# A fp32 transformer block on one Trainium2 core: a seventh-product form for three of eight k pairs in the feed-forward part

## The chip, the cores and the metric

The program runs on one core of one Trainium2 chip. The time is the device time of one execution in microseconds (us). Before the change three runs gave 1486.8, 1486.99 and 1487.1 us (median 1486.99). The profile is of one execution more, of 1487.96 us.

The engines are named as the profile names them: PE (matmuls; PEld is its weight load), DVE (elementwise on two operands), ACT (copies, casts, functions), POOL (here a few small operations and some transfers), SP (here only the queue of weight loads).

## The reference

One layer of a streaming encoder, all in fp32, for x of 256 x 2048 (256 tokens):

```
h = RMSNorm(x);  proj = h @ w_in                     # 2048 x 10240: q, k, v twice, two gates
y_sb = stick_breaking_attention(...)                  # 8 heads of 128
y_ca = chunked_relpos_attention(...)                  # 8 heads of 128
x += (sigmoid(g_sb) * (y_sb @ w_sb_out) + sigmoid(g_ca) * (y_ca @ w_ca_out)) @ w_mix_out
h = RMSNorm(x);  g, u = split(h @ w_ffn_in)           # 2048 x 11264
x += (silu(g) * u) @ w_ffn_out                        # 5632 x 2048
x += sigmoid(RMSNorm(x) @ w_ple_gate) * (p @ w_ple_in)
out = RMSNorm(x)
```

The change touches the two feed-forward products alone, `h @ w_ffn_in` and `(silu(g) * u) @ w_ffn_out`.

## The kernel before, in words

**How fp32 is kept.** PE multiplies in a reduced format (fp32r). Every fp32 operand is split into two tiles, hi (a cast) and lo (the rest), and a product is three matmuls, hi by hi, hi by lo and lo by hi (`three`, L254 to L256). A weight tile `raw` of 128 x 1024 (two k tiles of 128 rows by 512 columns, one transfer of 512 KB) comes in on SP's queue; ACT makes hi from it (L225) and DVE makes lo (L207, the helper `minus`). There are five raw buffers (`RAW`), and four pairs of hi and lo in the feed-forward part. The activations stand as tables of transposed tiles, T1, T2, T3, with hi and lo of each k tile.

**The feed-forward part** is cut into units. A unit multiplies all k tiles of a table with two weight blocks of 512 columns: for w_ffn_in the gate and the up columns of one group of 512 hidden features (16 k tiles, 8 pairs), for w_ffn_out two neighbouring groups of 512 output columns. The hidden features go in blocks (`FF_BLOCKS`, 16, 16 and 12 k tiles of 128): four, four and three units of w_ffn_in, each block followed by two units of w_ffn_out over its 16, 16 or 12 k tiles (8, 8 or 6 pairs). That makes 17 units. An ordinary pair has two weight blocks, two k tiles and two halves of the tokens: 8 products, 24 matmuls of 128 x 512.

**The 7-product form.** For the pairs in `PAIRS` (numbers 2 and 4 of each unit) the two k tiles and the two weight blocks are taken as a 2 x 2 matrix of blocks, and the eight products are replaced by seven of sums of blocks (`pair_products`), 21 matmuls. The price: DVE forms four sums of raw tiles, 128 x 512 each, (`split_pair`, written to `xf` and once in place to `raw`), ACT casts the three of them that are in xf (128 x 1536, L246), DVE takes their rest (`T<-xf,T`). The activation side needs the corresponding sums once per table (`forms` in `into_table`: four DVE additions `fm` of 128 x 128, a cast, a rest). Three of the seven products go straight into the unit's four result banks; four go into banks of their own, `su` (q1, q5, q6, q7). When the last such pair is done, `mid` (L792, L794) puts them together in the tile C: one ACT copy and four DVE additions. At the end of each weight block the result banks are added to C (L801, or L822 and L823), with silu and the product of gate and up behind (L805 to L810). PSUM has eight banks: four for the results of a unit and four for its su; the next unit swaps them, so its first results go to the banks that `mid` empties.

**Order.** The code records pieces in program order (`prefetch`, `split`, `products`): weights are loaded as far ahead as raw buffers are free, splits run up to three pieces ahead as far as hi and lo buffers reach. Small work (transposes of finished hidden features into a table, `into_table`) is put in `tasks` and run between pieces. A scheduler that plays the program through then sets the order on each engine, so rows of different pieces stand interleaved. Each engine runs its own list in order, and waits on the others by semaphores.

**Buffers that the change names.** T1 is free in the feed-forward part: its first 6144 columns are room for the casts of xf (two halves in turn), the rest holds `F_in`, the form tiles of the table of w_ffn_in. `F_out`, those of w_ffn_out, has a buffer with the tag "gf" that later holds the final gain vector `gf`. In the last two units the room is in T3.

Of the kernel before, what the change touches and what calls it, by code (L numbers as in the profile page):

```python
# [10 lines left out]
F32R = mybir.dt.float32r  # L11
# [5 lines left out]
P = 128  # L17
# [13 lines left out]
SCALE = P**-0.5  # L31
NB = 512
FB = 256
FF_BLOCKS = [16, 16, 12]

PAIRS = (2, 4)
RAW = 5


# [1 line left out]
def block_kernel(ctx: ExitStack, tc: tile.TileContext, x, p, w_in, w_sb_out, w_ca_out, w_mix_out,  # L41
# [18 lines left out]
    nc = tc.nc  # L60
# [65 lines left out]
    pieces = []  # L126
# [23 lines left out]
    def unit(wsrc, n0s, kts, lhs, forms, ext, mid, post, needs, row0=0):  # L150

        state["unit"] = state.get("unit", -1) + 1
        pool, side = late["ps"][:: 1 if state["unit"] % 2 == 0 else -1]
        g = dict(kind="unit", post=post, mid=mid, lhs=lhs, keep=None, forms=forms, ext=ext, pool=pool, side=side)
        kts = list(kts)
        for i in range(len(kts) // 2):
            part = kts[2 * i : 2 * i + 2]
            r = (row0 + 2 * i) * P
            src = [wsrc[r : r + 2 * P, n0 : n0 + NB].rearrange("(k p) n -> p k n", p=P) for n0 in n0s]
            pc = dict(g=g, kts=part, ncol=NB, needs=[needs(kt) for kt in part])  # L160
            if i in PAIRS:
                pieces.append(dict(pc, src=src, pair=True, first=i == PAIRS[0], last=i == PAIRS[-1]))
            else:
                for b in range(2):
                    pieces.append(dict(pc, src=[src[b]], block=b, first=i == 0, last=2 * i + 2 == len(kts)))
# [157 lines left out]
    late = {}  # L323
# [41 lines left out]
    def into_table(dst, c, src, gain=None, key=None, forms=None, pool=None):  # L365
# [3 lines left out]
        for k0 in range(0, 4, n):  # L369
# [7 lines left out]
            g = None if gain is None else [gT[:, gain + kt + k : gain + kt + k + 1] for k in range(n)]  # L377
            if forms is not None and kt // 2 in PAIRS:
                af = late["pool"].tile([P, 2, S], F32, tag="af", name="af", bufs=2)
# [289 lines left out]
    for mixer, make in ((0, sb_tasks), (1, ca_tasks)):  # L669
        for b in range(2):  # L670
# [3 lines left out]
            first = mixer == 0 and b == 0  # L674
# [75 lines left out]
    lp = ctx.enter_context(tc.tile_pool(name="late", bufs=1))  # L750
# [5 lines left out]


    flat = T1.rearrange("p k c s -> p (k c s)")
    F_in = flat[:, 6144:].rearrange("p (i c f s) -> p i c f s", i=len(PAIRS), c=2, f=4)
    F_out = lp.tile([P, len(PAIRS), 2, 4, P], F32R, tag="gf", name="F")  # L760
    late["F"] = [[F[:, i] for i in range(len(PAIRS))] for F in (F_in, F_out)]

    pt = lp.tile([P, NT, D_PLE], F32, tag="af", name="pt", bufs=2)
    dma_x.dma_start(pt, p[0, 0].rearrange("(t p) d -> p t d", p=P))
# [31 lines left out]
    def in_post(dst, c, key):  # L796
        def post(g, b):
            C = g["C"]
            for t in range(NT):
                i = 2 * b + t  # L800
                nc.vector.tensor_tensor(C[:, i, :], g["ps"][i], C[:, i, :], ALU.add)  # L801
            if b == 0:
                sg = lp.tile([P, NT, NB], F32, tag="sg", name="sg")
                for t in range(NT):
                    nc.scalar.activation(sg[:, t, :], C[:, t, :], AF.Sigmoid)  # L805
                for t in range(NT):
                    nc.vector.tensor_tensor(C[:, t, :], C[:, t, :], sg[:, t, :], ALU.mult)
            else:
                for t in range(NT):
                    nc.vector.tensor_tensor(C[:, t, :], C[:, t, :], C[:, 2 + t, :], ALU.mult)  # L810
                later(lambda: into_table(dst, c, C[:, :2, :], key=key, pool=g["pool"],
                                         forms=lambda kt: late["F"][1][kt // 4 - 1]))
        return post
# [17 lines left out]
    k0 = 0  # L831
    for blk, nk in enumerate(FF_BLOCKS):
        key = f"h{blk}"
        for c in range(nk // 4):
            j = k0 // 4 + c
            unit(w_ffn_in[0], (j * NB, D_FF + j * NB), range(KD), T3, lambda kt: late["F"][0][kt // 4 - 1], T1,
                 mid, in_post(T2, c, key), lambda kt: ("ffn", kt))
        last = blk == len(FF_BLOCKS) - 1
        for c in (0, 2):
            unit(w_ffn_out[0], (c * NB, (c + 1) * NB), range(nk), T2, lambda kt: late["F"][1][kt // 4 - 1],  # L840
                 T3 if last else T1, mid, out_unit_post(c, last), lambda kt, key=key: (key, kt), row0=k0)
        k0 += nk
# [6 lines left out]
    gf = lp.tile([P, D], F32, tag="gf", name="gf")  # L849
# [104 lines left out]
```

## Time and profile before

| what | value |
|---|---|
| profiled execution | 1487.96 us, span 1486.2 us |
| median of three runs | 1486.99 us (1486.8 to 1487.1) |
| PE busy | 1467.7 us, 99% of the span |
| DVE busy | 1071.5 us, 72% |
| ACT busy | 764.0 us, 51% |
| granted PE clock | 0.998, mean of the span |
| DMA | 289.07 MB, 195 GB/s in the mean |

Busy time is the union of an engine's intervals. The duration of one instruction is longer than the distance between two starts, since instructions of PE, and those of DVE, overlap their neighbours; so a duration times a count is not time on the engine, and distances between starts are read from the timeline. Waits name the engine and instruction that ended an idle time. A window gives the busy time of each engine in a stretch of the span. The feed-forward part runs from about 673 us to 1400 us of the span.

### The profile page before, as it was taken

The numbers are of one execution on the slowest core, as the hardware profiler recorded it, in microseconds if no ns is written. First come the engines' busy times: TensorE is split into PE (matmuls) and PEld (weight loads), VectorE is DVE, ScalarE is ACT, GpSimd is POOL, SyncE is SP. The second block draws the span as 40 slices with busy tenths as digits, with TensorE's granted clock in tenths as the row PEclk, the third lists the DMA queues.
The fourth block names the chain that finished last, engine by engine and source line by source line (L and its number), as shares of the span: only waits on it lengthen the run. The fifth ranks groups of instructions, "written<-read, shape, count | busy, mean of one in ns | idle before, by whom it ended". The sixth has DMA issues, their size and how long they took to land.

```text
span 1486.2 us, 18409 instructions
## 1 busy us (share of the span) xinstructions
PE 1467.7 (99%) x6922; PEld 1224.5 (82%) x6922; DVE 1071.5 (72%) x1291; ACT 764.0 (51%) x917; POOL 24.8 (2%) x45
## 2 busy tenths in 40 slices
PE   8999999999999999999999999999999999999997
PEld 6888888888888888887888888888888888887786
DVE  6667676665444566458888888888888888888875
ACT  6455554455454444457555544455454445555552
POOL 1100000000000000000000000000000000000000
PEclk9999999999999999999999999999999999999999
DMA  8855556556666666666666566666656666656672
GB/s 267 262 172 171 174 171 186 177 168 186 191 193 194 187 189 202 195 212 201 198 186 202 186 205 212 199 198 183 200 183 199 213 200 196 194 176 197 226 230 97
DMA packets 164810, 289.07 MB, mean 195 GB/s; under 512 B 9040, under 2 KB 44160, under 8 KB 164464
## 3 DMA queue, kind: packets, MB, share of 16 engines
q1 hardware_dynamic: 162560, 278.96, 60.7%
q0 software_dynamic: 2160, 8.93, 1.8%
q8 instruction: 54, 0.88, 0.2%
q14 instruction: 36, 0.29, 0.1%
HBM read 282.09 MB, written 5.77 MB: 194 GB/s over the span
## 4 chain that ended last, share of the span: by engine, by line
PE 91%; DVE 3%; DMA 2%; ACT 1%; issue 1%; SPq 0%; POOL 0%; POOLq 0%; DVEq 0%; ACTq 0%
PE mm L254 24%; PE mm L255 24%; PE mm L256 24%; PE mm L315 8%; PE mm L317 4%; PE su L255 2%; PE su L256 2%; PE su L254 2%; DVE lo L207 1%; DMA raw<-in_w_ffn_out 1%; PE tp L374 1%; DMA pin_d<-pst 1%; DVE T L207 0%; ACT hi L225 0%; DMA x<-in_x 0%
## 5 line engine op out<-in xcount | busy, mean ns | idle before, releaser
L207 DVE TENSOR_TENSOR lo<-raw,hi 128x1024 fp32r<-128x1024 f32 (+1 forms) x517 | 629.2, 1220 | 327.7 <-ACT hi L225 325.8
L225 ACT CAST hi<-raw 128x1024 fp32r<-128x1024 f32 (+1 forms) x449 | 471.6, 1051 | 534.9 <-PE mm L256 419.8
L255 PE MATMUL mm<-lo,T 128*128 128x512 f32 x1576 | 615.7, 391 | 0.0
L256 PE MATMUL mm<-hi,T 128*128 128x512 f32 x1576 | 614.5, 392 | 0.3 <-DVE T L402 0.3
L254 PE MATMUL mm<-hi,T 128*128 128x512 f32 x1576 | 588.0, 391 | 3.8 <-ACT hi L225 2.2
L254 PEld LDWEIGHTS mm<-hi,T 128*128 128x128 f32 x1576 | 296.0, 188 | 65.9 <-ACT hi L225 3.2
L255 PEld LDWEIGHTS mm<-lo,T 128*128 128x128 f32 x1576 | 296.4, 188 | 61.6 <-DVE lo L207 0.9
L256 PEld LDWEIGHTS mm<-hi,T 128*128 128x128 f32 x1576 | 296.2, 188 | 60.8 <-DVE T L402 0.7
L315 PE MATMUL mm<-T,hi 128*128 128x512 f32 x512 | 180.4, 399 | 0.0
L317 PE MATMUL mm<-T,lo 128*128 128x256 f32 x512 | 140.8, 280 | 0.0
L315 PEld LDWEIGHTS mm<-T,hi 128*128 128x128 f32 x512 | 95.3, 188 | 21.4
L317 PEld LDWEIGHTS mm<-T,lo 128*128 128x128 f32 x512 | 96.3, 189 | 1.1
L207 DVE TENSOR_TENSOR T<-xf,T 128x1536 fp32r<-128x1536 f32 x34 | 59.5, 1751 | 4.4 <-ACT T L246 4.3
L207 DVE TENSOR_TENSOR xf<-raw 128x512 f32<-128x512 f32 x68 | 46.5, 684 | 17.5 <-DMA raw<-in_w_ffn_out 8.8
L243 ACT CAST hi<-raw 128x1024 fp32r<-128x1024 f32 x34 | 35.9, 1057 | 39.1 <-PE mm L256 26.3
L246 ACT CAST T<-xf 128x1536 fp32r<-128x1536 f32 x34 | 50.4, 1482 | 10.3 <-DVE xf L207 10.2
L794 DVE TENSOR_TENSOR C<-su,C 128x512 f32<-128x512 f32 x68 | 45.3, 687 | 11.5 <-PE su L256 9.5
L240 ACT CAST hi<-raw 128x1024 fp32r<-128x1024 f32 x34 | 36.1, 1061 | 25.1 <-PE mm L256 19.5
L801 DVE TENSOR_TENSOR C<-mm,C 128x512 f32<-128x512 f32 x44 | 29.9, 682 | 0.0
L360 ACT COPY tm<-mm 128x256 f32<-128x256 f32 x32 | 11.9, 372 | 24.2 <-PE mm L317 24.2
L255 PE MATMUL mm<-T,T 128*128 128x512 f32 (+1 forms) x66 | 24.1, 365 | 0.1
L254 PE MATMUL mm<-T,T 128*128 128x512 f32 (+1 forms) x66 | 24.1, 365 | 0.0
(223 smaller groups left out, 1045.0 us busy)
## 6 DMA issues: line engine op xcount, KB each, us to landing
raw<-in_w_ffn_in SPq DMA_DIRECT2D x176, 512.0 KB, 4.3
raw<-in_w_in SPq DMA_DIRECT2D x159, 512.0 KB, 3.6
raw<-in_w_ffn_out SPq DMA_DIRECT2D x88, 512.0 KB, 4.7
raw<-in_w_mix_out SPq DMA_DIRECT2D x32, 512.0 KB, 4.6
raw<-in_w_ple_gate SPq DMA_DIRECT2D x32, 512.0 KB, 5.0
raw<-in_w_sb_out SPq DMA_DIRECT2D x16, 512.0 KB, 4.5
raw<-in_w_ca_out SPq DMA_DIRECT2D x16, 512.0 KB, 4.2
raw<-in_w_ple_in SPq DMA_DIRECT2D x4, 512.0 KB, 4.6
```

The lines of the kernel that those rows point to most:

```text
L207: nc.vector.tensor_tensor(out, a, b, ALU.subtract)
L225: nc.scalar.copy(hi[:, c : c + m], raw[:, c : c + m])
L240: nc.scalar.copy(h1, raw1)
L243: nc.scalar.copy(h2, raw2)
L246: nc.scalar.copy(xh, xf)
L254: nc.tensor.matmul(ps, xh, hi, start=a, stop=False)
L255: nc.tensor.matmul(ps, xh, lo, start=False, stop=False)
L256: nc.tensor.matmul(ps, xl, hi, start=False, stop=z)
L315: nc.tensor.matmul(ps, hi[:, i, f], lhs[:, kt, :, :].rearrange("p c s -> p (c s)"), start=a, stop=False)
L317: nc.tensor.matmul(ps[:, :S], lo[:, i, f], lhs[:, kt, 0, :], start=False, stop=z)
L794: nc.vector.tensor_tensor(C[:, i, :], q, C[:, j, :], ALU.add)
L801: nc.vector.tensor_tensor(C[:, i, :], g["ps"][i], C[:, i, :], ALU.add)
```

## The change

`PAIRS` becomes (2, 4, 6), and a unit takes those numbers that are smaller than its last pair: 2, 4 and 6 of 8, as before 2 and 4 of 6. The blocks come in the order 12, 16, 16. The form tiles of w_ffn_in, now three, get the buffer with the tag "gf"; those of w_ffn_out lie in T1 behind its first 6144 columns (two) and in a new buffer of 4 KB per partition (the third). The scratch for descriptors of DMAs that POOL starts is set to 8192 bytes.

```diff
-FF_BLOCKS = [16, 16, 12]
-
-PAIRS = (2, 4)
+FF_BLOCKS = [12, 16, 16]
+
+PAIRS = (2, 4, 6)
...
-            if i in PAIRS:
-                pieces.append(dict(pc, src=src, pair=True, first=i == PAIRS[0], last=i == PAIRS[-1]))
+            taken = [j for j in PAIRS if j < len(kts) // 2 - 1]
+            if i in taken:
+                pieces.append(dict(pc, src=src, pair=True, first=i == taken[0], last=i == taken[-1]))
...
-    F_in = flat[:, 6144:].rearrange("p (i c f s) -> p i c f s", i=len(PAIRS), c=2, f=4)
-    F_out = lp.tile([P, len(PAIRS), 2, 4, P], F32R, tag="gf", name="F")
-    late["F"] = [[F[:, i] for i in range(len(PAIRS))] for F in (F_in, F_out)]
+    F_in = lp.tile([P, 3, 2, 4, P], F32R, tag="gf", name="F_in")
+    F_out = flat[:, 6144:].rearrange("p (i c f s) -> p i c f s", i=2, c=2, f=4)
+    F_more = lp.tile([P, 2, 4, P], F32R, tag="fo", name="F_more")
+    late["F"] = [[F_in[:, i] for i in range(3)], [F_out[:, 0], F_out[:, 1], F_more]]
...
-    nc = bacc.Bacc("TRN2", target_bir_lowering=False, num_devices=1)
+    nc = bacc.Bacc("TRN2", target_bir_lowering=False, num_devices=1, dynamic_dma_scratch_size=8192)
```

In the built programs PE has 5890 matmuls of 128 x 512 before and 5845 now. On DVE the additions that fill xf go from 68 and 34 to 98 and 49, those into raw from 34 to 49, the rests `T<-xf,T` from 34 to 49; on ACT the casts `T<-xf` go from 34 to 49. The activation side has a form step more for three tables: the additions `fm` go from 32 to 44. POOL's and SP's lists hold the same transfers; on POOL the load of `gf` now stands ahead of the first two loads of `pi` and not behind them. Line numbers of the changed kernel are one higher from about L160 on and two higher from about L760 on.

Two places show what moves. The first is DVE around `mid` (the rows `C<-su`) in a unit of w_ffn_in. `lo<-raw,hi` is the rest of an ordinary weight tile, `xf<-raw` and `raw<-raw` are sums for the next 7-product pair, `C<-mm` adds a result bank at the end of a weight block. Before:

```order
L207 TENSOR_TENSOR T_71<-xf,T_71 128x1536
L207 TENSOR_TENSOR lo<-raw,hi 128x1024 x3
L794 TENSOR_TENSOR C<-su_8041,C 128x512
L794 TENSOR_TENSOR C<-su_8042,C 128x512
L794 TENSOR_TENSOR C<-su_8040,C 128x512 x2
L207 TENSOR_TENSOR lo<-raw,hi 128x1024 x4
L801 TENSOR_TENSOR C<-mm_7942,C 128x512
L207 TENSOR_TENSOR xf<-raw 128x512
```

And in the changed program:

```order
L208 TENSOR_TENSOR T_71<-xf,T_71 128x1536
L208 TENSOR_TENSOR lo<-raw,hi 128x1024 x2
L208 TENSOR_TENSOR xf<-raw 128x512
L796 TENSOR_TENSOR C<-su_8283,C 128x512
L208 TENSOR_TENSOR raw<-raw 128x512
L796 TENSOR_TENSOR C<-su_8284,C 128x512
L803 TENSOR_TENSOR C<-mm_8175,C 128x512
L208 TENSOR_TENSOR xf<-raw 128x512
L796 TENSOR_TENSOR C<-su_8282,C 128x512 x2
L208 TENSOR_TENSOR lo<-raw,hi 128x1024
```

The four additions of `mid` have moved to the end of the unit. They stand among the sums for the next unit's first 7-product pair, one of them (`xf<-raw`, which waits for a weight tile of the next unit) in front of the first, and among the additions of the result banks.

The second place is PE from the last products into the su banks (of q6 and q7) on. `mm_7943` and `mm_8176` are result banks of the same unit. Before:

```order
L255 MATMUL su_8041<-T_71 128x512
L256 MATMUL su_8041<-T_71 128x512
L255 MATMUL su_8042<-T_71 128x512
L256 MATMUL su_8042<-T_71 128x512
L255 MATMUL mm_7943<-T_71,T_4848 128x512
L256 MATMUL mm_7943<-T_71,T_4848 128x512
L254 MATMUL mm_7943<-hi,T_4848 128x512
```

In the changed program, where `mm_8524` is the second result bank of the next unit:

```order
L257 MATMUL su_8284<-T_71,F_in 128x512
L256 MATMUL mm_8176<-T_71,T_4848 128x512
L257 MATMUL mm_8176<-T_71,T_4848 128x512
L255 MATMUL mm_8176<-hi,T_4848 128x512
L256 MATMUL mm_8176<-lo,T_4848 128x512
L257 MATMUL mm_8176<-hi,T_4848 128x512
L255 MATMUL mm_8176<-hi,T_4848 128x512
L256 MATMUL mm_8176<-lo,T_4848 128x512
L257 MATMUL mm_8176<-hi,T_4848 128x512
L255 MATMUL mm_8524<-hi,T_72 128x512
```

Before, 66 rows of the same unit stand between the last product into an su bank and the first of the next unit. Now there are eight, the rest of pair 7, before the first matmul that waits for `mid`: `mm_8524` waits for the first of the four additions, a matmul 6 places later for the second, and one 20 places later for the last.

## The prediction

> **What bounds the kernel now.** I began with the page, whose first part says PE, then asked stage by stage where PE stands still.
>
> ```profile
> PE 1467.7 (99%) x6922; PEld 1224.5 (82%) x6922; DVE 1071.5 (72%) x1291; ACT 764.0 (51%) x917; POOL 24.8 (2%) x45
> 655.00:700.00 45.00, 43.90 (x207) 35.70 (x206) 34.57 (x53) 36.51 (x59) 3.49 (x5) 1.00 0.63 204
> 700.00:1345.00 645.00, 645.00 (x2890) 534.36 (x2889) 541.81 (x624) 328.93 (x341) 0.00 (x0) 1.00 0.64 197
> 1345.00:1405.00 60.00, 56.57 (x256) 44.53 (x255) 51.87 (x72) 34.76 (x55) 2.72 (x4) 1.00 0.64 214
> ```
>
> A window's row is the stretch, its length, busy time of PE, PEld, DVE, ACT and POOL, the granted PE clock, the DMA share and GB/s. In the 645 us that hold nearly the whole feed-forward part PE is busy without a gap at clock 1.00, and DVE is busy for 541.81 us, 84%. PE stands still 1.1 us on the way in and 3.4 us on the way out. So in this stage a matmul less is time less, as long as DVE follows. What one costs is the distance between starts:
>
> ```profile
> 1032.71 0.39 PE L255 MATMUL mm<-lo,T 128*128 128x512 f32 x1
> 1032.94 0.39 PE L256 MATMUL mm<-hi,T 128*128 128x512 f32 x1
> 1033.16 0.39 PE L254 MATMUL mm<-hi,T 128*128 128x512 f32 x1
> 1033.39 0.39 PE L255 MATMUL mm<-lo,T 128*128 128x512 f32 x1
> 1024.91:1068.01 43.10, 43.10 (x196) 35.71 (x195) 37.64 (x48) 23.49 (x26) 0.00 (x0) 1.00 0.65 202
> 1161.45:1203.61 42.16, 42.16 (x187) 34.92 (x187) 35.14 (x40) 20.02 (x19) 0.00 (x0) 1.00 0.67 207
> ```
>
> Three starts lie 0.68 us apart, 0.227 us each. The last rows are one unit of w_ffn_in (with eight transposes) and one of w_ffn_out: 42.16 / 186 matmuls gives 0.2267 us again.
>
> **What is removed.** All 11 units of w_ffn_in and the four long units of w_ffn_out get one more 7-product pair, three matmuls less each: 45 x 0.2267 = **-10.2 us**. A unit of w_ffn_in then takes 43.10 - 0.68 = 42.42 us of PE, a long one of w_ffn_out 41.48.
>
> **What is added lies on DVE and ACT.** DVE's queue, where it is full, shows its prices as distances between starts:
>
> ```profile
> 1024.86 0.68 DVE L810 TENSOR_TENSOR C<-C 128x512 f32<-128x512 f32 x1
> 1025.46 1.22 DVE L207 TENSOR_TENSOR lo<-raw,hi 128x1024 fp32r<-128x1024 f32 x1
> 1026.60 1.75 DVE L207 TENSOR_TENSOR T<-xf,T 128x1536 fp32r<-128x1536 f32 x1
> 1028.26 1.22 DVE L207 TENSOR_TENSOR lo<-raw,hi 128x1024 fp32r<-128x1024 f32 x1
> 1031.74 0.28 DVE L389 TENSOR_TENSOR fm<-af 128x128 f32<-128x128 f32 x1
> 1031.94 0.28 DVE L207 TENSOR_TENSOR fm<-af 128x128 f32<-128x128 f32 x1
> 1032.14 0.68 DVE L207 TENSOR_TENSOR T<-tp,T 128x512 fp32r<-128x512 f32 x1
> 1044.47 2.81 DVE L794 TENSOR_TENSOR C<-su,C 128x512 f32<-128x512 f32 x4 [0.36 <-PE su L256]
> 1050.09 1.22 DVE L207 TENSOR_TENSOR lo<-raw,hi 128x1024 fp32r<-128x1024 f32 x1 [1.05 <-ACT hi L225]
> 1052.81 1.22 DVE L207 TENSOR_TENSOR lo<-raw,hi 128x1024 fp32r<-128x1024 f32 x1 [1.50 <-ACT hi L225]
> ```
>
> That is 0.60 us for 512 columns, 1.14 for 1024, 1.66 for 1536, 0.20 for 128. A 7-product pair adds four sums and one rest, 4 x 0.60 + 1.66 = 4.06 us. A full unit of w_ffn_in then asks of DVE 16 x 1.14 = 18.2 (lo), 3 x 4.06 = 12.2 (pairs), 2.7 (mid), 8 x 0.60 = 4.8 (ends of the blocks), 2 x 0.60 = 1.2 (table) and 4 x 0.20 + 0.60 = 1.4 (form): **40.5 us of PE's 42.4**, 96%. A unit of w_ffn_out asks 18.2 + 12.2 + 2.7 + 4.8 = 37.9 of 41.5. The cover is what DVE now idles in each unit, 43.10 - 37.64 = 5.5 us, mostly as in the last two rows: between pair 5 and the unit's end DVE waits for hi, and ACT for PE to give up a buffer. Those idles come after need is met, so the new work may fill them; without that cover each unit would lose up to 4.06 us. ACT gets a cast of 1536 more (mean 1.48 us) on 20 to 23 us of 42, which hides. Weight traffic is unchanged.
>
> **Does it fit in time, not only in sum?** The strain is the unit's end, where `mid` now stands with only pair 7 left. From the built order: after the last su product PE has 8 matmuls, 1.8 us, until it needs the first op of `mid`, 14 (3.2 us) until the second, 28 (6.3 us) until the last. If DVE stands ready, these end 0.6, 1.8 and 4.2 us after (between them a sum and a block end of 0.60 each, then another two): 1.2, 1.4 and 2.1 us to spare. From there to the rest `T<-xf,T` of the next unit's pair 2 the queue has 4 ops of mid, 3 sums, 4 block ends, one silu product, two lo and the rest: 12 x 0.60 + 2 x 1.14 + 1.66 = 11.1 us, and PE wants it 57 matmuls, 12.9 us, after the last su product. It fits by 1 to 2 us each time.
>
> One op can spoil that: `xf<-raw` ahead of `mid`, which needs a weight tile of the next unit. Its transfer starts when the next unit's first lo is done; 1.66 + 2 x 1.14 = 3.9 us of other DVE work follow, and the landing takes 4.3 to 4.7:
>
> ```profile
> raw<-in_w_ffn_in SPq DMA_DIRECT2D x176, 512.0 KB, 4.3
> raw<-in_w_ffn_out SPq DMA_DIRECT2D x88, 512.0 KB, 4.7
> SPq L191 <- DVE lo L207: 482.6, 217, 6.4
> ```
>
> So DVE waits up to 1 us there, while it mostly waits for the su products anyway. The third row, the loads' own queue between 700 and 1350 us, says that loads always start when DVE gives up a tile: a late DVE makes late loads. The trace of before has the same picture once, in the short units with 6 pairs, where only pair 5 follows `mid`:
>
> ```profile
> 1340.83 2.35 DVE L207 TENSOR_TENSOR lo<-raw,hi 128x1024 fp32r<-128x1024 f32 x2
> 1345.84 0.69 DVE L794 TENSOR_TENSOR C<-su,C 128x512 f32<-128x512 f32 x1 [2.67 <-PE su L256]
> 1348.76 0.69 DVE L207 TENSOR_TENSOR xf<-raw 128x512 f32<-128x512 f32 x1 [2.23 <-DMA raw<-in_w_ffn_out]
> 1353.44 1.28 DVE L794 TENSOR_TENSOR C<-su,C 128x512 f32<-128x512 f32 x2
> 1385.54 1.49 DVE L794 TENSOR_TENSOR C<-su,C 128x512 f32<-128x512 f32 x2 [2.25 <-PE su L256]
> 1362.98 0.50 PE L255 MATMUL mm<-lo,F 128*128 128x512 f32 x1 [0.32 <-DVE lo L207]
> 1374.76 0.50 PE L254 MATMUL mm<-hi,T 128*128 128x512 f32 x1 [2.20 <-ACT hi L225]
> ```
>
> There the tile landed 6.8 us after the lo that freed its buffer (1341.97 to 1348.76), `mid` ended 9 us after it began, and yet PE lost 0.3 us in the next 20. The 2.2 us at 1374.76 come behind a load of 8.9 us, in the stretch that also makes the table for the last stage. Round the second short `mid`, at 1385.54, no PE wait is shown. Per unit the stall is thus bounded by 0 and, if the 2.2 us returned each time, 2.2. I take 0.1, nearest to these two units (0.3 and 0): **+1.5 us** for 15.
>
> **The way in.** There the first unit's splits and the table of w_ffn_in share DVE and ACT, and the chain of waits runs over them up to the start of PE's row:
>
> ```profile
> 694.87 1.05 ACT hi L225
> 695.96 0.50 PE mm L254
> ```
>
> ```profile
> 673.00:704.00 31.00, 30.57 (x140) 24.75 (x141) 28.41 (x42) 24.78 (x39) 0.69 (x1) 1.00 0.56 178
> ```
>
> In the window from 673 to 704 us DVE is idle for 2.6 us. The table's third form adds 4 x 0.20 + 0.60 + 0.60 of DVE and saves two of its 0.40 steps: 1.2 us. Bounds 0 and 2.5 (with ACT's 1.1 and a wait); I take **+1.2**. **The way out** keeps its shape, with a long unit in the short one's place: 0, between -3.4 (all PE waits there gone) and +3.
>
> **At nothing:** the order of the blocks (same units, same sums), the form tiles' places, the smaller scratch. POOL's transfers lie off PE's path; the load of gf waited 21 us for its buffer before and is now earlier. If the scratch held up POOL, the cover would be the stretches in which POOL only waits:
>
> ```profile
> POOL gf L850 <- PE su L256: 21.0, 1, 21.0
> POOL bias L622 <- DVE sm L362: 169.8, 1, 169.8
> ```
>
> **Sum:** 1487.96 - 10.2 + 1.5 + 1.2 = 1480.5 us for a profiled execution; the median of the runs shown lies 0.97 lower than that execution: **1479.5 us**.
>
> **Rivals.** (a) *DVE's queue is blocked ahead of `mid`* (slower). Where the tile for `xf` lands 2.2 us after DVE could use it, as at 1348.76, and that is after the su products, the first op of `mid` ends 2.2 + 0.6 + 0.6 = 3.4 us behind them; PE had 1.8, so it stands 1.6 us in each of 15 units: 1487.0 - 10.2 + 1.2 + 24 = 1502. From 0.6 us a unit on (10.2 - 1.2 over 15) the gain is gone. For it: the op's place; against: the transfer starts early enough to be about level with the su products, and the short units lost 0.3. (b) *DVE is the bound.* By durations (1.22, 1.75, 0.68, 0.28 and 2.81) instead of distances the unit of w_ffn_in asks 19.5 + 3 x 4.47 + 2.8 + 5.4 + 1.4 + 1.8 = 44.3 us, 1.2 over today's 43.10; 11 such, and four units of w_ffn_out 0.7 under: 1487.0 + 13.2 - 2.7 = 1497.5. The rows above speak against it: starts lie closer than durations. (The Trainium skill, page "VectorE: DVE Perf Modes", section "The DRAIN you can't avoid", says that an op does not start before the one ahead has left the pipe, and excepts ops that are not held; the overlap in the rows is that exception.) (c) *Stalls of 0.3 to 0.9 us a unit*, single tiles that come late: 1482.5 to 1490. (d) *All fits and the way out gains too*: 1487.0 - 10.2 - 3.4 = 1473.4. (e) That the change does not do what it says is out: the built lists have the 45 matmuls less.
>
> (The Trainium skill, page "TensorE: Matmul & The Clock Gate", Part 1, has PE's clock halved after about 3.4 us of idling; at the 2.2 us idle before 1374.76 the window's clock is 1.00, and no run here shows a longer one within the stage.)
>
> **Numbers.** Forecast (1476 to 1482.5) 0.66, (d) 0.07, (c) 0.15, (a) 0.07, (b) 0.05. The range 1475.5 to 1488 leaves out (a), (b), a quarter of (c) and most of (d), 0.2 in all. What this kernel's measurement can tell from no change is about 0.2%, 3 us: faster below 1484.0. Faster: forecast, (d) and half of (c) but a little, 0.80; same: the rest of (c), 0.08; slower: (a) and (b), 0.12.
>
> **What would show it.** Right: PE busy throughout the long window, matmuls at 0.227 us, DVE near 93% there, waits of PE on DVE and ACT under 2 us in sum between 705 and 1345. Wrong by (a): each unit shows a PE wait at the second result bank, ended by `C<-su`, with `xf` waiting for a DMA ahead of it. Wrong by (b): DVE without a gap for whole units, PE waiting for lo or `T<-xf,T`. Wrong on the way in: a PE wait over 2.5 us between 673 and 705.

## The result, and the profile after

The changed kernel takes **1510.7 us** (four runs, 1509.4 to 1511.2) against 1487.05 of the kernel before on the same chip: 1.0155 times, 95% interval 1.0142 to 1.0168. 1479.5 was forecast, with a range of 1475.5 to 1488. The profiled execution took 1511.01 us, its span is 1509.3.

First the busy times from the page of the kernel after; then the windows that were shown of before (way in, long stretch, way out).

```profile
PE 1470.7 (97%) x6877; PEld 1213.6 (80%) x6877; DVE 1130.8 (75%) x1380; ACT 780.9 (52%) x938; POOL 24.9 (2%) x45
```

```profile
655.00:700.00 45.00, 45.00 (x216) 37.43 (x215) 36.53 (x56) 36.93 (x59) 3.50 (x5) 1.00 0.67 213
700.00:1345.00 645.00, 626.91 (x2749) 505.12 (x2748) 581.11 (x691) 333.54 (x350) 0.57 (x1) 1.00 0.60 191
1345.00:1405.00 60.00, 53.44 (x235) 43.18 (x234) 49.57 (x61) 33.25 (x44) 1.45 (x2) 0.94 0.57 183
```

The matmuls are fewer, as planned, and PE still loses. In the 645 us it started 2749 instructions, before 2890: 141 x 0.2267 = 32 us less work in the same time. Only 18 us of that show as idle time, since starts that lie a little further apart still overlap. DVE is busy for 581 us, 90%: fuller than before, and not full. Who waited for whom between 705 and 1345 us:

```profile
ACT hi L226 <- DMA raw<-in_w_ffn_in: 61.8, 22, 5.0
ACT hi L226 <- PE mm L257: 37.8, 26, 4.1
ACT hi L226 <- DMA raw<-in_w_ffn_out: 30.6, 9, 6.1
PE mm L255 <- DVE C L796: 10.4, 8, 3.7
DVE xf L208 <- DMA raw<-in_w_ffn_out: 9.4, 5, 5.9
DVE xf L208 <- DMA raw<-in_w_ffn_in: 7.0, 8, 2.2
PE mm L255 <- ACT hi L226: 3.2, 6, 1.1
PE mm L256 <- DVE lo L208: 3.0, 4, 1.1
```

(Columns: us in total, times, longest.) ACT, which makes hi, now waits 92 us for weight tiles to land; before, there was only DVE's wait of 14 us at `xf`. PE's longest waits are for `C<-su`, the ops of `mid`, at 8 of the 15 ends of units in this stretch. The timeline around one `mid`, of ACT, DVE and PE:

```profile
1046.75 1.05 ACT L226 CAST hi<-raw 128x1024 fp32r<-128x1024 f32 x1 [3.16 <-DMA raw<-in_w_ffn_out]
1047.83 1.23 DVE L208 TENSOR_TENSOR lo<-raw,hi 128x1024 fp32r<-128x1024 f32 x1 [1.94 <-ACT hi L226]
1050.07 0.69 DVE L208 TENSOR_TENSOR xf<-raw 128x512 f32<-128x512 f32 x1 [1.01 <-DMA raw<-in_w_ffn_out]
1050.68 0.68 DVE L796 TENSOR_TENSOR C<-su,C 128x512 f32<-128x512 f32 x1
1051.42 0.50 PE L255 MATMUL mm<-hi,T 128*128 128x512 f32 x1 [2.08 <-DVE C L796]
```

and from the chain of waits there four links, of which the second landing is that of the tile for `xf`:

```profile
1030.64 4.60 DMA raw<-in_w_ffn_in
1036.40 1.23 DVE lo L208
1043.11 6.86 DMA raw<-in_w_ffn_out
1050.68 0.68 DVE C L796
```

The su products were done by 1048. DVE stood twice for tiles ahead of `mid`, and PE then stood 2.08 us for `mid`. The tiles come late since DVE gave their buffers up late: the second load starts at 1043.11, as a lo ends. In this unit it is the picture of rival (a), and the first theory made of it ("late tiles") is that five raw buffers don't suffice for three pairs. Its rivals: "full DVE" (DVE's work is simply too much) and the rest of the change (order of blocks, form tiles, scratch).

### The profile page after: what moved, and what is told of

Its sections match the earlier page's. It is cut to its first block, busy times and chain, and to the rows that moved or that the text cites. A ratio compares the mean times of both kernels' runs of the same rounds, so it can differ in the third digit from the quotient of the medians.

```text
span 1509.3 us, 18436 instructions
## 1 busy us (share of the span) xinstructions
PE 1470.7 (97%) x6877; PEld 1213.6 (80%) x6877; DVE 1130.8 (75%) x1380; ACT 780.9 (52%) x938; POOL 24.9 (2%) x45
## 4 chain that ended last, share of the span: by engine, by line
PE 62%; DVE 19%; DMA 10%; issue 6%; ACT 3%; SPq 0%; POOL 0%; DVEq 0%; POOLq 0%; ACTq 0%
PE mm L255 15%; PE mm L257 15%; PE mm L256 15%; DVE lo L208 8%; PE mm L316 8%; DMA raw<-in_w_ffn_in 5%; DMA raw<-in_w_ffn_out 5%; PE mm L318 4%; DVE xf L208 3%; ACT hi L226 2%; DVE C L796 1%; DVE T L208 1%; DVE C L803 1%; DVE raw L208 1%; PE su L255 1%
## 5 line engine op out<-in xcount | busy, mean ns | idle before, releaser
L226 ACT CAST hi<-raw 128x1024 fp32r<-128x1024 f32 (+1 forms) x419 | 438.0, 1050 | 477.6 <-PE mm L257 250.2
L256 PE MATMUL mm<-lo,T 128*128 128x512 f32 x1461 | 571.7, 392 | 1.7 <-DVE lo L208 1.6
L255 PE MATMUL mm<-hi,T 128*128 128x512 f32 x1461 | 548.9, 394 | 21.0 <-DVE C L796 11.4
L257 PE MATMUL mm<-hi,T 128*128 128x512 f32 x1461 | 567.8, 391 | 0.1
L255 PEld LDWEIGHTS mm<-hi,T 128*128 128x128 f32 x1461 | 274.8, 188 | 87.5 <-DVE C L796 13.8
L256 PEld LDWEIGHTS mm<-lo,T 128*128 128x128 f32 x1461 | 274.7, 188 | 61.3 <-DVE lo L208 5.3
L257 PEld LDWEIGHTS mm<-hi,T 128*128 128x128 f32 x1461 | 274.5, 188 | 56.9 <-DVE T L403 0.5
L208 DVE TENSOR_TENSOR T<-xf,T 128x1536 fp32r<-128x1536 f32 x49 | 85.8, 1752 | 4.7 <-ACT T L247 4.5
L247 ACT CAST T<-xf 128x1536 fp32r<-128x1536 f32 x49 | 72.6, 1482 | 31.5 <-DVE xf L208 31.5
L208 DVE TENSOR_TENSOR xf<-raw 128x512 f32<-128x512 f32 x98 | 67.2, 686 | 18.7 <-DMA raw<-in_w_ffn_out 10.0
L244 ACT CAST hi<-raw 128x1024 fp32r<-128x1024 f32 x49 | 51.5, 1050 | 50.6 <-DVE raw L208 24.5
L241 ACT CAST hi<-raw 128x1024 fp32r<-128x1024 f32 x49 | 51.4, 1050 | 25.0 <-PE su L257 14.0
L208 DVE TENSOR_TENSOR xf<-raw,xf 128x512 f32<-128x512 f32 x49 | 33.6, 686 | 0.4
L208 DVE TENSOR_TENSOR raw<-raw 128x512 f32<-128x512 f32 x49 | 33.5, 684 | 0.3
```

What stands on the lines that cost most here:

```text
L208: nc.vector.tensor_tensor(out, a, b, ALU.subtract)
L226: nc.scalar.copy(hi[:, c : c + m], raw[:, c : c + m])
L241: nc.scalar.copy(h1, raw1)
L244: nc.scalar.copy(h2, raw2)
L247: nc.scalar.copy(xh, xf)
L255: nc.tensor.matmul(ps, xh, hi, start=a, stop=False)
```

## The experiments

Ratios are to the kernel before, in runs on the same chip (its median was 1487.0 to 1488.8 us there, so times of different rows compare to about 1 us); brackets hold 95% intervals. Edits are to the changed kernel if nothing else is said. Each edit lets the scheduler plan the lists anew; what an edit shows holds with that.

One measure of the traces comes up several times, the *due time* of `mid`: how many matmuls PE still has between its last su product and the first matmul that waits for DVE to release one of the banks that `mid` empties. In the changed kernel it is 13 in eight of the long units, 8 in four (the unit shown ahead of the prediction is one of them) and 19 in three. A small number is an early due time.

**Six tiles, with three pairs and with the kernel before.**

```diff
-RAW = 5
+RAW = 6
...
-dynamic_dma_scratch_size=8192
+dynamic_dma_scratch_size=4096
```

> The changed kernel with six raw weight buffers in place of five (the scratch for POOL's transfers goes to 4096 bytes to make room). Late tiles: if DVE loses its time at instructions whose weight tile has not landed, because a tile's load starts only when DVE has given up the one five loads before, a sixth buffer starts each load some 2.5 us of DVE work earlier, more than half of a landing of 4.4 us; most of the 33 us lost against 1477 comes back: 1478 to 1490. Full DVE: if DVE is simply too full (40.5 us of work in 42.4) the buffer changes little: 1503 to 1512.

Measured: **1473.7 us**, 0.9895 [0.988, 0.991]; the fastest of the kernels that compute the reference. Long window, and waits from 705 to 1345 us:

```profile
700.00:1345.00 645.00, 644.03 (x2888) 531.97 (x2887) 609.12 (x728) 357.32 (x377) 2.02 (x3) 1.00 0.63 200
ACT hi L226 <- PE mm L257: 129.9, 84, 5.1
PE mm L255 <- DVE C L796: 0.4, 2, 0.2
```

DVE is busy for 94% of the time and PE still runs without loss, so full DVE falls as a cause by itself. ACT now waits for PE to release hi buffers and no longer for tiles: PE sets the pace. `mid` is due as early as in the changed kernel, after 13 matmuls in most units. Against the changed kernel the sixth tile is worth 37.0 us, 2.5 us for each of 15 long units.

> The kernel before with six raw buffers and the scratch of 8192 bytes. Both theories: PE had no wait in its long stretch, so 1484 to 1488. A gain here would mean that the ring was short before the change too; a loss that the smaller scratch or the new addresses cost something.

The kernel before with `RAW = 6` and the scratch of 8 KB: 1482.9, 0.9959 [0.9943, 0.9975], some 6 us, a little more than expected; the stalls on the way in and out go (PE busy 45.00 of 45 and 59.62 of 60 us).

**Two pairs, and three pairs without their sums.**

```diff
-PAIRS = (2, 4, 6)
+PAIRS = (2, 4)
```

> The changed kernel with PAIRS back at (2, 4): the order 12, 16, 16, the places of the form tiles and the scratch of 8192 bytes stay. Late tiles and full DVE: 1484 to 1490, since the third pair makes the loss. Third theory, that the order of the blocks, the new buffers or the scratch make it: over 1495.

1483.2, 0.9959 [0.9944, 0.9974]: the rest of the change gains, and the third pair costs 27.5 us. The way in and the way out of this run:

```profile
655.00:700.00 45.00, 45.00 (x215) 37.10 (x214) 36.46 (x54) 37.13 (x59) 3.50 (x5) 1.00 0.67 212
1345.00:1405.00 60.00, 59.68 (x279) 49.36 (x278) 46.75 (x60) 34.06 (x50) 2.07 (x3) 1.00 0.67 215
```

```diff
+        if pc["kts"][0] == 12:
+            (h1, l1), (h2, l2) = buffers(1024), buffers(1024)
+            nc.scalar.copy(h1, raw1)
+            nc.scalar.copy(h2, raw2)
+            minus(l1, raw1, h1.bitcast(F32))
+            minus(l2, raw2, h2.bitcast(F32))
+            ...
+            return
```

> The changed kernel with the third pair's matmuls (21 in place of 24), but without its four sums, its cast of 1536 and its rest: the seven products take the unsummed tiles, so this pair's result is left wrong. Late tiles and full DVE: PE's 45 matmuls less are worth 10.2 us and nothing stands against them: 1475 to 1480. If the sparing of matmuls is worth less than counted, or the place of the sums step behind pair 6 costs PE by itself: 1483 or more.

This one keeps the 21 matmuls of the third pair and leaves out its sums, their cast and rest (PE multiplies h1, h2, l1 and l2 in their place, so the products of that pair are not the reference's). 1472.9: 10.3 us under two pairs. Long window, and PE's only wait for `mid` from 705 to 1345 us:

```profile
700.00:1345.00 645.00, 643.43 (x2888) 532.21 (x2887) 555.97 (x660) 336.90 (x365) 2.02 (x3) 1.00 0.63 202
PE mm L264 <- DVE C L805: 1.6, 1, 1.6
```

PE's saving is as counted; all of the loss comes with the sums, their cast and their rest. `mid` stands behind pair 6 here too and is due after 11 or 12 matmuls in nine of the 15 long units (28 in the others): an early due time with two pairs' work on DVE costs nothing.

**Scratch alone**, in the kernel before.

> The kernel before with the scratch of 8 KB alone. The changed kernel with two pairs took 0.41% less than before, though it does the same work: either the scratch or the order of the blocks (short one first) with the new places of the form tiles. If the scratch does it, 0.9945 to 0.9975 of before; if the order of the blocks does, 0.999 to 1.001.

1487.7, 1.0001 [0.9991, 1.001]: nothing. What two pairs gain thus comes from the order of the blocks and the places of the form tiles, which no run takes apart.

**The op ahead of mid.** The first two sums of a pair are held behind the last op of the `mid` ahead of them:

```diff
-        minus(t3, b[1][:, 1, :], b[1][:, 0, :])
-        minus(b[1][:, 0, :], b[1][:, 0, :], b[0][:, 0, :])
+        if "mid" in state:
+            with tc.issue_after(state["mid"].ins):
+                minus(t3, b[1][:, 1, :], b[1][:, 0, :])
+                minus(b[1][:, 0, :], b[1][:, 0, :], b[0][:, 0, :])
...
```

> The changed kernel with one order forced on DVE: the first two sums of a 7-product pair (xf<-raw and raw<-raw) are issued only behind the last op of the mid that stands before them, so no tile of the next unit can hold up mid any more. Five tiles as before. Late tiles as a matter of place (my rival (a): DVE's queue blocked ahead of mid): the waits of PE for C<-su go, and most of the 27 us that the third pair costs against the same kernel with two pairs come back: 1475 to 1490. Late tiles as a matter of the ring (five tiles; every lo that comes late starts the next load late, wherever DVE stands in its list): the waits move to hi and lo, the time stays between 1498 and 1520. Full DVE (which the sixth tile spoke against): 1505 or more.

1505.0, 1.0112 [1.0097, 1.0127]. Waits from 705 to 1345 us:

```profile
ACT hi L226 <- DMA raw<-in_w_ffn_in: 71.0, 24, 4.7
PE mm L260 <- DVE C L801: 2.8, 4, 1.5
```

DVE no longer waits for DMA at `xf`, PE waits 2.8 us for `mid` in place of 10.4, and only 5.7 us come back. Rival (a), with that op as the cause, falls. ACT's waits for landings are longer than before (the row and 41.4 us for w_ffn_out), so PE's own stalls at `mid` are not most of the loss.

**DVE's work without a pair**, in the kernel before (with the scratch of 8 KB): 4 x 512 and 1 x 1536 columns subtracted on a constant, ahead of the lo of k tiles 12 and 13 in each long unit.

```diff
+                for w in (4, 4, 4, 4) if pc["block"] == 0 else (12,):
+                    d = nc.vector.tensor_tensor(dump[:, : w * P], one.to_broadcast((P, w, P)), one.to_broadcast((P, w, P)), ALU.subtract)
```

> The kernel before, with scratch of 8 KB, and on DVE alone the work that the third pair adds, put where that pair's sums would stand: ahead of the splits of k tiles 12 and 13 of each of the 15 long units, four subtractions of 512 columns and one of 1536 on a constant, into a tile of their own that nothing reads. No weight tile is held by them, the matmuls are those of before, and ACT gets nothing. If the loss comes from DVE's lateness alone (a late lo starts the next load late, and a ring of five has no slack for it), this costs as much as the third pair cost beside its saving, 27 + 10 us, or somewhat less, since the pair's two tiles come free one by one: 1505 to 1525. If it needs the pair (both tiles held until the sums and both casts are through, ACT's 1536-wide cast), the work fills DVE's idle time: 1484 to 1490. In between, 1491 to 1504, both have a share.

1485.1, 0.9985 [0.9975, 0.9994]. Long window and the added ops:

```profile
700.00:1345.00 645.00, 644.60 (x2881) 532.21 (x2880) 596.03 (x697) 327.00 (x341) 0.00 (x0) 1.00 0.62 196
L229 DVE TENSOR_TENSOR dump<-ones 128x512 f32<-128x512 f32 x57 | 39.0, 684 | 0.5
L229 DVE TENSOR_TENSOR dump<-ones 128x1536 f32<-128x1536 f32 x15 | 26.2, 1748 | 0.0
```

The same DVE work as that of the third pair costs nothing when it stands in a kernel with two pairs. DVE is busy for 92% of the window, a little under the 94% of three pairs: PE keeps its 24 matmuls at that place, so a unit has 0.68 us more room, and `mid` is due as late as in the kernel before.

**The same work, now on the pair's two tiles**, so that it needs both landed and holds both.

```diff
+                if pc["block"] == 0:
+                    raw2, = pieces[state["split"] + 1]["raw"]
+                    for u, v in ((raw2, raw2), (raw2, raw), (raw2, raw2), (raw, raw2)):
+                        d = minus(dump[:, :NB], u[:, NB:], v[:, :NB])
```

> As the run with work on DVE alone (1485.1), with one thing changed: the four subtractions of 512 columns now read the two weight tiles of k tiles 12 and 13 (first the second one), as the sums of a pair do, so that they can't start before both have landed and neither lo can give its tile up before they are through. PE and ACT do what they did. The kernel with the sums read from a constant showed that DVE's time alone costs nothing here. If the loss of the changed kernel comes from the pair's need of two landed tiles out of five, it comes back here: 1498 to 1520. If it does not (it comes from where mid and the ends of the blocks pile up at the unit's end, or from the order of the whole list), 1483 to 1491.

1485.7, 0.9986 [0.9977, 0.9995]: nothing either.

**Four tiles and six with two pairs** (`RAW = 4`; `RAW = 6` with the scratch of 4 KB).

> The changed kernel with two pairs in each long unit and four tiles for incoming weights in place of five. With five it took 1483.2. If the ring decides, one tile less takes away some 2.7 us of lead from each load, as the third pair's work on DVE did, and the loss is of the same kind: ACT's hi waits for DMA in every unit, time 1505 to 1560. If five tiles had a margin with two pairs, it stays under 1490.

> The changed kernel with two pairs in each long unit, six tiles and scratch of 4 KB. With five tiles it took 1483.2, with three pairs and six tiles 1473.7. If five tiles were enough for two pairs, the sixth brings nothing here: 1482 to 1484, and the third pair is worth its 10.2 us of matmuls once the tiles are there (1473.7 against this run). If the sixth tile helps in its own right, 1474 to 1480, and the third pair is worth less than counted.

1484.1 with four tiles, 1483.2 with five, 1481.1 with six. With four tiles ACT waits 30 us for landings between 705 and 1345 us, most of it before 905 us, and PE does not mind. The longest of these rows, and PE's wait for lo:

```profile
ACT hi L226 <- DMA raw<-in_w_ffn_in: 21.1, 17, 3.6
PE mm L256 <- DVE lo L208: 0.8, 2, 0.5
```

"Five tiles are too few" is thus no property of the ring by itself: with two pairs even four do. Late tiles are the form that the loss takes; what makes them late is still open here.

**Other places for the three pairs.** With 2, 3 and 4 the short units keep two:

```diff
-PAIRS = (2, 4, 6)
+PAIRS = (2, 3, 4)
...
-            taken = [j for j in PAIRS if j < len(kts) // 2 - 1]
+            taken = [j for j in PAIRS if j < len(kts) // 2 - 2]
```

> The changed kernel with the three 7-product pairs at places 2, 3 and 4 of the eight, in place of 2, 4 and 6 (in the short units 2 and 3). Number of sums, products, tiles and bytes is the same; mid now stands three pairs ahead of the unit's end, as in the kernel before, and so its four ops don't fall together with the block ends, the products with silu and the next unit's first sums. If that pile-up, 11 us of DVE's list in which few tiles are given up, starves the five tiles, the gain returns: 1472 to 1484. If a third pair as such is too much for five tiles, the loss stays or grows (three pairs behind one another): 1498 to 1530.

1529.4, 1.028 [1.0263, 1.0297]: 18.7 us slower than the changed kernel, although `mid` is due later than there (after 39 matmuls or more in every long unit). Three pairs in a row cost more than three spaced ones; no run with six tiles tells whether the ring of five is the reason here.

> The changed kernel with the three pairs at places 1, 3 and 5 (in the short units 1 and 3), so mid has two pairs of single tiles behind it in place of one, but the next unit's first sums come two tiles earlier. If the pile-up at the unit's end decides, about half of the loss goes: 1482 to 1500. If a third pair as such is too much for five tiles, 1500 to 1520.

With `PAIRS = (1, 3, 5)`: **1481.2**, 0.9951 [0.9935, 0.9968]. The distances between pairs are 2, 2 and 4 as with 2, 4, 6; the work is the same, and 29.5 us of the loss are gone. Its long window, and waits from 705 to 1345 us:

```profile
700.00:1345.00 645.00, 640.93 (x2859) 526.34 (x2858) 605.41 (x724) 354.54 (x369) 1.26 (x2) 1.00 0.62 199
ACT hi L226 <- PE mm L257: 167.7, 75, 6.1
ACT hi L226 <- DMA raw<-in_w_ffn_out: 6.0, 3, 4.1
```

What differs is where the unit's end lies. `mid` comes after the last pair; with 2, 4, 6 one pair of single tiles is left to PE (24 matmuls, 5.4 us) before the next unit's first product needs a bank that `mid` must have emptied; with 1, 3, 5 there are two. The scheduler takes part of that ahead of the last su product, so the due times in the traces are 8 to 19 matmuls (1.8 to 4.3 us) with 2, 4, 6 and 19 to 44, mostly 27 (6.1 us), with 1, 3, 5.

**A pile-up at the unit's end, or a due time?** With 1, 3, 5, `mid` was held behind the lo of the next unit's first tile, so that in DVE's list it stands among the ends and the next sums:

```diff
-        if z:
-            g["mid"](g)
...
+                    behind = pieces[state["at"] + 2 :][:1]
+                    if behind and "end" in behind[0]:
+                        with tc.issue_after(behind[0]["end"].ins):
+                            g["mid"](g)
```

> The three pairs at places 1, 3, 5 (1481.2 with mid four single tiles ahead of the unit's end), and mid's ops now forced behind the lo of the next unit's first tile, so that they stand among the block ends and the next unit's first sums, as in the changed kernel. Nothing else differs. If the pile-up at the unit's end is what costs, the loss comes back: 1495 to 1525. If the place of the pairs among the tiles decides, and mid doesn't, it stays: 1478 to 1486.

1480.5: no loss. The place in DVE's list isn't it. The due time stayed late here, 27 matmuls or more in the long units, so the run says nothing of that. Then the products with silu and the additions to x were put on POOL (`nc.gpsimd` for `nc.vector` in three lines), and in a second run four subtractions of 512 columns put back ahead of k tile 6 of every unit (with the scratch of 4 KB):

> The changed kernel (pairs 2, 4, 6, five tiles) with the products with silu and the additions to x, four ops of 512 columns in each unit just behind mid, on POOL in place of DVE. If the pile-up costs, most of the 28 us return: 1472 to 1490. If the place of the third pair among the tiles costs, the end of the unit isn't where it is lost, and 1500 to 1515 remains.

> As the run before, and four subtractions of 512 columns on a constant put back on DVE in each unit, ahead of the split of k tile 6, half a unit away from its end (scratch 4 KB for the room they write to, which nothing reads). DVE's total is that of the changed kernel again. If the ends on POOL help by the place where they stood, this stays within 6 us of the run before. If they help because DVE has less to do in all, it goes back towards the changed kernel: 1498 to 1512.

1508.9 and 1547.2; neither theory expected the second. They don't tell what they were made for, because DVE was not relieved (below, in the last section). What the first does show: with DVE slowed, a late due time doesn't save the kernel, since the scheduler left 22 to 30 matmuls to `mid` in all but one of the long units whose due time the trace shows. But four subtractions more, 4 x 0.60 = 2.4 us, in each of the 17 units cost 38.3 / 17 = 2.3 us a unit here, where in the kernel before 4.06 us cost nothing. With DVE slowed by POOL as well, its time lies on the path that sets the end; that the same holds without POOL is not shown.

**The due time taken away.** ACT copies all four su results out of their banks; DVE's four additions stay, now within C.

```diff
-        nc.scalar.copy(C[:, 0, :], q1)
-        for i, q, j in ((2, q6, 0), (1, q7, 2), (3, q5, 1), (2, q5, 2)):
-            nc.vector.tensor_tensor(C[:, i, :], q, C[:, j, :], ALU.add)
+        for i, q in ((0, q1), (2, q6), (1, q7), (3, q5)):
+            nc.scalar.copy(C[:, i, :], q)
+        for i, j in ((2, 0), (1, 2), (2, 3), (3, 1)):
+            nc.vector.tensor_tensor(C[:, i, :], C[:, i, :], C[:, j, :], ALU.add)
```

> The changed kernel (pairs 2, 4, 6, five tiles) with mid in another form: ACT copies all four su results out of their banks into C (it copied one), and DVE then makes the same four additions within C. DVE's ops keep their number and width; ACT gets three copies of 512 columns, 0.57 us each, a unit. The next unit's first products write the banks of su, so they now wait for ACT and no longer for DVE. What decides is then told apart: if it is mid's due time (with the pairs at 2, 4, 6 only one pair of single tiles, 24 matmuls or 5.4 us, lies between the last su product and the next unit's first product; with 1, 3, 5 twice that), PE's waits for C<-su go and most of the 28 us return: 1474 to 1490. If the five tiles are short by themselves at these places, PE waits for hi and lo instead, 1500 to 1515.

**1490.2** (ten runs, 1486.6 to 1494.3), 1.0014 [1.0003, 1.0025]: 20.5 us come back with the same pairs, tiles and DVE ops. Long window, and waits from 705 to 1345 us:

```profile
700.00:1345.00 645.00, 635.48 (x2821) 519.91 (x2820) 595.51 (x706) 368.12 (x408) 0.57 (x1) 1.00 0.63 197
ACT hi L226 <- DMA raw<-in_w_ffn_in: 43.2, 16, 5.4
ACT hi L226 <- DMA raw<-in_w_ffn_out: 9.6, 5, 3.9
PE mm L256 <- DVE lo L208: 5.6, 7, 1.2
```

No PE wait for `mid` is left; some of the waits for tiles are.

**Late mid alone.** Pairs 2 and 6 in the long units:

```diff
-            taken = [j for j in PAIRS if j < len(kts) // 2 - 1]
+            taken = [2, 6] if len(kts) == 16 else [2, 4]
```

> The changed kernel with the pair at place 4 taken out of the long units, so that two pairs stand at 2 and 6: mid is as late as with 2, 4, 6 (one pair of single tiles before the next unit's first product), but DVE has the work of two pairs only. With pairs at 2 and 4 it took 1483.2. If mid's late due time costs by itself, 1490 to 1505 (half or more of the 20 us that ACT's copies brought back). If it costs only where DVE is nearly full, so that a list that has fallen behind never comes forward again, 1481 to 1486.

1482.2, 0.9952 [0.9936, 0.9969]: no loss. Its long window, and two waits from 705 to 1345 us; then, from its timeline, a last su product, three ops of `mid`, and the first matmul that needs a bank from them:

```profile
700.00:1345.00 645.00, 643.81 (x2882) 532.60 (x2881) 547.32 (x646) 331.84 (x350) 0.57 (x1) 1.00 0.63 197
DVE xf L208 <- DMA raw<-in_w_ffn_in: 27.4, 19, 3.7
DVE xf L208 <- DMA raw<-in_w_ffn_out: 24.8, 9, 4.5
1031.42 0.39 PE L257 MATMUL su<-T,F_in 128*128 128x512 f32 x1
1033.16 2.00 DVE L796 TENSOR_TENSOR C<-su,C 128x512 f32<-128x512 f32 x3
1038.45 0.39 PE L255 MATMUL mm<-hi,T 128*128 128x512 f32 x1
```

DVE waits 52 us at `xf` for tiles, more than in the changed kernel, and makes it up each time.

But the run does not do what it was made for. `mid` stands behind pair 6 in the program; in PE's order all 24 matmuls of pair 7 come behind the last su product, and `mid` is due after 29 or 30 matmuls, 7.0 us, in every long unit where the trace shows it (1031.42 to 1038.45 above, with `mid` through at 1035.16). That is later than with 1, 3, 5. The due time follows from how the scheduler plans the whole list, not from the last pair's number alone; what tests an early one with two pairs' work on DVE is the run without sums, where it cost nothing.

**The best places with six tiles.**

> Three pairs at places 1, 3, 5 with six tiles and scratch of 4 KB. With five tiles this order took 1481.2, of which about 8 are still above the PE sum; with places 2, 4, 6 six tiles took 1473.7. If six tiles remove what is left of the waits, 1472 to 1475, no better than places 2, 4, 6; if the next unit's first sums, two tiles after its start, hold something up that no tile cures, 1476 to 1481.

1475.6, 0.9911 [0.9895, 0.9928], not better than 2, 4, 6 with six tiles (1473.7).

## Why the prediction was wrong

With five tiles the runs stand in a square (us; the pairs' places in brackets):

| `mid` due, in matmuls behind the last su product | DVE's work of two pairs | DVE's work of three pairs |
|---|---|---|
| 19 or more, mostly 27 and over | 1483.2 (2, 4); 1482.2 (2, 6) | 1481.2 (1, 3, 5); but 1529.4 (2, 3, 4) |
| mostly 8 to 13 | 1472.9 (2, 4, 6 without the third pair's sums, 10.2 us less for PE) | **1510.7** (2, 4, 6) |

With the pairs spaced and nothing moved to POOL, neither a nearly full DVE nor an early due time of `mid` costs much alone; together, with five tiles, they do. Pairs in a row (2, 3, 4) and a DVE slowed by POOL (1508.9) lose with a late due time as well, so this pairing is one way to the loss and not the only one. Each of three edits takes most of the changed kernel's loss away: another place for the pairs (29.5 us), the banks emptied by ACT (20.5), a sixth tile (37.0). This much is shown. How the conditions work together is read from the waits and is argued: where nothing holds it up, DVE keeps ahead even with three pairs, and ACT mostly waits for PE (129.9 us with six tiles and 167.7 with 1, 3, 5). With 40.5 us of work in 42.4 it recovers little of a delay. It then comes to the next `mid` late, PE stands, DVE gives its tiles up late, the loads start late, and DVE must idle for landings, which is time that it hasn't got. PE's stalls at `mid` are only one link of this, as the run with the sums held behind `mid` shows (2.8 us of them left, 1505.0). In the timeline of after, the 14 distances from one long unit's first op of `mid` back to that of the unit before come to 627.9 us, where PE's work is 10 x 42.42 + 4 x 41.48 = 590.1: 2.7 us a unit, near the 37.0 / 15 = 2.5.

Step by step:

- *Less PE work, -10.2 us:* right (10.3 between the run without sums and two pairs; 7.4 between three and two pairs with six tiles, which is 2.8 us short of it).
- *DVE's added work fits, 40.5 of 42.4 us:* right as a sum, and as a load: the same work put beside two pairs was free, and a DVE that was busy for 94% lost nothing with six tiles.
- *"I take 0.1, nearest to these two units (0.3 and 0): +1.5 us for 15"*: **this step failed.** Measured 2.5 us a unit, 37 in all (changed kernel against six tiles), beyond the bound of 2.2. The two units that it leaned on are short ones: their `mid` is due as early, after 18 and 13 matmuls, but they have two pairs of six, and a delay there was followed by next to no loss. The run without sums shows that an early due time without the third pair's work tells nothing of the case with it. The fit was also worked out for a DVE that "stands ready" at the su products; in the trace shown it had been waiting for tiles, with one lo between, since 1045.9. And the cover, 5.5 us of DVE idle in each unit, was counted as free time to be filled. With pairs at 2, 4, 6 and five tiles it seems to be what brought DVE forward again; this is the argued part.
- *Way in +1.2, way out 0:* PE lost nothing on the way in, with the scratch alone neither (busy 45.00 of 45 us). On the way out PE stands idle for 6.6 us in the changed kernel, with two pairs for 0.3, before for 3.4.
- *Order of the blocks, form tiles and scratch at nothing:* the scratch yes; the other two together gain 0.4% with two pairs. The size of it was named for the way out as a bound (-3.4).
- *Rival (a):* right in sign, and its time of 1502 is the nearest. Its line ("a PE wait at the second result bank, ended by `C<-su`, with `xf` waiting for a DMA") is to be seen at 1051.42, but not in each unit: PE waits for `C<-su` 8 times between 705 and 1345 us, 10.4 us in all, where (a) asked for 24. Wrong in its cause: without that op ahead of `mid` 1505.0 remain, so that its time is near is luck. *Rival (b)*, DVE as the bound by its durations, fell with 94% busy at no loss. *(c)* and *(d)* are out with the sign; (d)'s time, 1473.4, happens to be near that of six tiles. ((c)'s upper end is a slip: 0.9 us a unit give 1491.5 and not 1490.)

Open stay: why three pairs in a row (2, 3, 4) lose still more though `mid` is due late there; how much of the loss is the due time and how much the late tiles, which no run separates; what the last 7.5 us of 1, 3, 5 against 2, 4, 6 with six tiles are, of which a sixth tile brings 5.6 (1475.6); and whether the 20.5 us of ACT's copies and the rest up to 37 are one loss or two.

## What to carry to other kernels

When an engine that serves the bottleneck goes from 84 to 94% of its time, test its fit with what brings it forward again after a delay, not with the sum: evidence for "a stall here costs nothing" from a stretch in which it had time to spare does not carry over. Look for the due time with the least cover (here the banks that pass from one unit to the next) and put the added work where that is loose; here a place one pair earlier was worth 29.5 us at no price. And read the due time from the order that was built: the program text said that pairs at 2 and 6 make it early, the built order did not. One more buffer of input is an insurance whose worth depends on the rest: 2.1 us with two pairs (some 6 in the kernel before), 5.6 with three at 1, 3, 5 and 37.0 with three at 2, 4, 6.

## What the runs showed of the hardware

**PE's clock.** A long stall costs more than its length. On the way out of the changed kernel PE waits 5.6 us, and the next starts lie 0.43 us apart for 3.5 us, then 0.23 again; the window's granted clock is 0.94 (above).

```profile
1379.34 0.39 PE L257 MATMUL mm<-hi,T 128*128 128x512 f32 x1
1385.35 0.79 PE L255 MATMUL mm<-hi,T 128*128 128x512 f32 x1 [5.62 <-ACT hi L226]
1385.94 0.63 PE L255 MATMUL su<-hi,T 128*128 128x512 f32 x1
1386.37 0.63 PE L256 MATMUL su<-lo,T 128*128 128x512 f32 x1
1388.84 0.40 PE L255 MATMUL mm<-hi,T 128*128 128x512 f32 x1
1389.08 0.40 PE L256 MATMUL mm<-lo,T 128*128 128x512 f32 x1
```

From 1385.35 to 1388.84 eight matmuls start where 15 would, some 1.7 us lost. The rule of the Trainium skill named in the prediction ("TensorE: Matmul & The Clock Gate", Part 1, half clock after about 3.4 us of idling and full clock after as much work) agrees with these rows.

**POOL beside DVE.** With the ends on POOL, DVE had some 60 ops fewer in the long window (633 for 691) and was busier than in the changed kernel, 594.0 us for 581.1. The ops of lo, of the changed kernel (first row) and with the ends on POOL, and POOL's products:

```profile
L208 DVE TENSOR_TENSOR lo<-raw,hi 128x1024 fp32r<-128x1024 f32 x233 | 279.2, 1218 | 41.0 <-ACT hi L226 40.4
```

```profile
L208 DVE TENSOR_TENSOR lo<-raw,hi 128x1024 fp32r<-128x1024 f32 x233 | 301.6, 1312 | 0.0
L809 POOL TENSOR_TENSOR C<-C,sg 128x512 f32<-128x512 f32 x22 | 35.6, 1624 | 383.3 <-ACT sg L807 383.3
1003.08 1.71 DVE L208 TENSOR_TENSOR lo<-raw,hi 128x1024 fp32r<-128x1024 f32 x1
1003.91 2.04 POOL L809 TENSOR_TENSOR C<-C,sg 128x512 f32<-128x512 f32 x1 [0.20 <-ACT sg L807]
1004.72 1.78 DVE L208 TENSOR_TENSOR raw<-raw 128x512 f32<-128x512 f32 x1
```

A sum of 512 columns takes 1.78 us in place of 0.69 while POOL runs, a lo 1.71 in place of 1.22; over the window the same 233 lo ops are 22 us longer, and the sums `xf<-raw` and `raw<-raw` 21 us, which is more than the 58 x 0.60 = 35 us taken off DVE. The Trainium skill, page "SBUF — State Buffer", section "Who interferes with whom", says that a DVE instruction with two SBUF inputs contends with a POOL instruction that reads SBUF; the sums and lo, which read two tiles in SBUF, agree.
